# Padding and shifting the weight slots of a two-block transformer kernel, so that weight tiles begin at a chosen distance behind the activation rows modulo 512 bytes

## The chip, the cores and the metric

One core of one Trainium2 chip. The metric is the device time of one execution in microseconds, as the median over runs. The profile is of one execution, traced on that core.

## What is computed

The reference runs two different blocks one behind the other on 256 tokens of width 1024, all in float32. What matters here is which products there are:

```
block 1:  xn = rms_norm(x);  proj = xn @ w_in            # 1024 x 4608
          y  = stick-breaking attention, retention       # small products
          h  = x + (g_sb*y_sb + g_ret*y_ret) @ w_out     # gates: xn @ w_gate
          h  = h + mixture of 16 experts (top 2 of one group of 4)
block 2, two layers, 256 tokens of x and 256 of a context:
          h += 0.5*gate * swiglu(modulate(rms_norm(h)), ffn1_up, ffn1_down)   # 1024 -> 2x2816 -> 1024
          h += gate * (neighbourhood | pool | grouped attention of (a @ w_in)) @ w_out
          h += 0.5*gate * swiglu(..., ffn2_up, ffn2_down)
```

In the second layer's last feed-forward the context is no longer needed, so only 256 tokens are left.

## The kernel before, in words

**Products.** Each large product is made from two-way split operands, so that float32 accuracy is kept with the fast number format: a weight w is split into wH (rounded) and wL (the rest), an activation x into xH and xL, and the sum wH·xH + wH·xL + wL·xH is formed. `gemm` (lines 235 to 244) issues these three matmuls for each block of 128 contraction rows, lines 241, 242 and 243; each has a 128x128 weight tile that TensorE loads (LDWEIGHTS, shown as PEld) and 256, 258 or 512 activation columns that it streams (MATMUL, shown as PE). The next matmul's weight tile is loaded while the matmul before it streams.

**Weights.** `rows` and `load` bring 1 MB of raw weights by DMA from SyncE's queue. `split_w` (lines 220 to 229) takes a slot of 2,048 columns per partition from the pool of weight slots, writes wH into its first half with ScalarE (line 225) and wL into its second half with VectorE or GpSimd (line 228). A slot holds 8 blocks of 128 columns (or 4 of 256, or 2 of 512) in each half, so every 128-column weight tile in a slot begins a multiple of 512 bytes behind the slot's beginning. The slots rotate: 4 in block 1 (`wsp1`), 2 in the mixture of experts (`wspe`), 4 from the first feed-forward to the end (`wsp`).

**Activations.** xH and xL (`setup`, lines 395 and 396) are 8 rows of 512 columns (2,048 bytes) each; tokens of x are columns 0 to 255, the context's are 256 to 511. In the feed-forward (`ffn`, line 569) the up products read xH and xL into `pab`, and the down products read the hidden tiles hH and hL into `pd`. The feed-forward runs over four parts of 6, 6, 6 and 4 hidden blocks (`PARTS`); the first up group of a feed-forward goes through `first` (line 246), which computes the two 256-column halves one after the other while the other half's norm is still being applied; in the very first feed-forward the second part (`EARLY`) has the context's half done already in the mixture of experts (`early_ffn`), so it streams 256 columns. The last down part streams 256 columns at a time. The last feed-forward (`late`) has one 256-column half and two more columns in front of it: 258 columns, beginning at column 254 of the row (line 586). `mix` (line 1308) makes `pj` (from w_in) and `po` (from w_out): 512 columns wide where both halves are needed, with two column groups of w_in again through `first`.

**Order of work.** The program is written as generators that are interleaved by hand (`blend`, `side`, `advance`): while TensorE works on a feed-forward, VectorE computes pieces of the next modulation vectors (`ada`, line 539), a few after each up group. Nothing in that order reads a tile's address.

**Where the tiles lie.** Tiles are placed one behind the other in a partition, in the order of their pools. In the kernel before, in bytes from the partition's beginning:

| tiles | begin at | modulo 512 |
|---|---|---|
| xH, xL, rows of 2,048 bytes | 36,480 and 52,864 | 128 |
| first of 4 weight slots, 8,192 bytes each (block 1, and from the first feed-forward on) | 119,776 | 480 |
| behind these slots: hidden tiles hH, hL (feed-forward), or ysH, ysL (block 1's attention output) | 152,544, 162,784 | 480 |
| `mix`: stacked queries qs (used as weights) / split keys kH, kL (streamed) | 203,168 / 192,736 | 416 / 224 |
| mixture of experts: hidden tiles eH, eL of `early_ffn` | 136,160 | 480 |
| mixture of experts: first of 2 weight slots | 166,432 | 32 |

Between xL and the first weight slot lie, in this order, the small constants, three raw buffers and the scratch pool.

Of the kernel before, what the change touches and what calls it, by code (L numbers as in the profile page):

```python
# [8 lines left out]
F32 = mybir.dt.float32  # L9
F32R = mybir.dt.float32r  # L10
# [19 lines left out]
SB_PACE, RET_PACE, ADA_PACE = 0.8, 0.8, 0.6  # L30
QK_PACE, NA_PACE, OUT_PACE = (2.25, 1.25), (0.75, 0.8), 0.5
NEG = -1e30

_INS = [
    "x", "norm_mix_g", "w_in", "w_gate", "b_gate", "w_sb_out", "w_ret_out", "ret_norm_g", "w_out",
# [134 lines left out]
class Builder:  # L170
    def __init__(self, tc, I, out, ctx):
        self.tc, self.I, self.out, self.ctx = tc, I, out, ctx
        self.nc = tc.nc
        self.const = self.pool("const", 1)
        self.raw = self.pool("raw", 3)
        self.scr = self.pool("scr", 7)
        self.ps = self.pool("ps", 1, space=PSUM)
        self.raw_more, self.raw_loop, self.raw_n = None, None, 0
        self.on_pool, self.mark, self.later, self.spare = 0, None, [], []
        self.pending, self.early, self.norm_a2 = iter(()), iter(()), False  # L180

    def pool(self, name, bufs, **k):
# [34 lines left out]
    def rows(self, w, r0, k, c0, cols):  # L217
        return self.load(w[r0:r0 + 128 * k, c0:c0 + cols].rearrange("(k p) c -> p k c", p=128), k, cols)

    def split_w(self, v):  # L220
        k, cols = v.shape[1], v.shape[2]
        r = lambda t: t[:, :k * cols].rearrange("p (k c) -> p k c", c=cols)
        w = self.wsp.tile([128, 2, 1024], F32R, tag="w", name="w")
        wh, wl = r(w[:, 0, :]), r(w[:, 1, :])
        self.nc.scalar.activation(wh, v, AF.Copy)  # L225
        self.on_pool = (self.on_pool << 1 | self.on_pool >> 3) & 15
        e = self.nc.gpsimd if self.on_pool & 1 else self.nc.vector
        e.tensor_tensor(wl, v, wh.bitcast(F32), ALU.subtract)  # L228
        return wh, wl
# [156 lines left out]
    def setup(self):  # L386
        nc, I = self.nc, self.I
        C = self.const
        sqc = C.tile([128, 896], F32, name="sqc")
        nc.scalar.dma_start(sqc[:, :256], I["k_sq"][:, :256])  # L390
        self.sqc = sqc
        self.ident, self.ones, self.tri, self.perm1, self.perm2, self.flip, self.before = (
            sqc[:, i * 128:(i + 1) * 128] for i in range(7))
        self.h = C.tile([128, KD, T2], F32, name="h")
        self.xH = C.tile([128, KD, T2], F32R, name="xH")
        self.xL = C.tile([128, KD, T2], F32R, name="xL")
        xs = self.token_tiles(I["x"])
        vr = self.vector_rows()
        self.vectors(*vr)
        self.first_norm(xs)  # L400
        self.sT = C.tile([128, KD, 64], F32, name="sT")
        nc.vector.memset(self.sT, 0.0)
# [174 lines left out]
    def ffn(self, l, n, up, dn, vs, side, pace, after):  # L577
# [3 lines left out]
        with ExitStack() as st:  # L581
# [3 lines left out]
            late = len(vs) == 1  # L585
# [4 lines left out]
            f0 = 0  # L590
            for pi, nf in enumerate(PARTS):
                hid = []
                full_n = 256 * len(vs)
                N = 256 if l + n == 0 and pi == EARLY else full_n
                full = slice(0, N)
                for c in range(nf // 2):
                    c0 = (f0 + 2 * c) * 128
                    va = self.rows(up, 0, KD, c0, 256)
                    vb = self.rows(up, 0, KD, NFF * 128 + c0, 256)
                    todo, pabs = [], []  # L600
                    for i in range(2):
# [4 lines left out]
                            p = self.a2("pab")  # L606
                            p = [p[:, 0, :], p[:, 1, :]]
                        pabs.append(p)
                        todo.append((self.split_w(va[:, :, cs]), p[0]))
                        todo.append((self.split_w(vb[:, :, cs]), p[1]))  # L610
                        if pi == 0 and c == 0 and i == 0:
                            continue
                        if late:
# [33 lines left out]
                if pi < len(PARTS) - 1:  # L647
                    for dc in range(4):
                        v = self.rows(dn, f0 * 128, nf, dc * 256, 256)
                        for i in range(2):  # L650
                            w = self.split_w(v[:, :, i * 128:(i + 1) * 128])
                            p = self.mm("pd")
                            self.gemm(p[:, full], w, lambda f: hid[f])
                            for v2 in range(N // S):
                                self.residual(p[:, half(v2)], 2 * dc + i, l, n, v2)
                        for _ in range(pace[1] if N == full_n else 1):
                            next(side, None)
                else:
                    ws = [self.split_w(self.rows(dn, f0 * 128, nf, dc * 256, 256)) for dc in range(4)]
                    for v in sorted(vs):  # L660
                        sq = []
                        for d in range(KD):
# [304 lines left out]
    def moe(self):  # L967
        nc, I = self.nc, self.I
        V = nc.vector
        self.raw_n, self.raws = 0, 7  # L970
        with self.sub("hn", 1) as Q, self.sub("hide", PARTS[EARLY]) as E, self.sub("moe", 1) as P, \
                self.sub("wspe", 2) as self.wsp, self.sub("moew", 1) as W, self.sub("rawm", 4) as self.raw_more:
            hH = [Q.tile([128, 1024], F32R, name=f"hnH{t}") for t in range(2)]
# [332 lines left out]
    def mix(self, l):  # L1306
        nc, I = self.nc, self.I
        full = l == 0
        w_in = I["w_in_2"][l]
        NX = 512 if full else 256  # L1310
        with self.sub("mx", 1) as P, self.sub("mxw", 2) as W:
# [2 lines left out]

            def weights(c):
                v = self.rows(w_in, 0, KD, c * 256, 256)
                return [self.split_w(v[:, :, i * 128:(i + 1) * 128]) for i in range(2)]

            first = []
            self.on_pool = 5  # L1320
# [94 lines left out]
            def most():  # L1415
                for c in range(4):
                    v = self.rows(I["w_out_2"][l], 256, 6, c * 256, 256)
                    for i in range(2):
                        w = self.split_w(v[:, :, i * 128:(i + 1) * 128])
                        n = NX  # L1420
                        if full and c == 3:
                            n = S
# [313 lines left out]
    def run(self):  # L1736
# [3 lines left out]
        self.moe()  # L1740
        self.wsp = self.pool("wsp", 4, reuse_waits="tile")

        for l in range(2):
            side = self.adas((0, 1), (0, 2)) if l == 0 else self.adas((1, 2))
            self.ffn(l, 0, I["ffn1_up_2"][l], I["ffn1_down_2"][l], (1, 0) if l == 0 else (0, 1), side, (5, 3),
# [33 lines left out]
```

## Time and profile before

| | |
|---|---|
| runs | 2264.26, 2265.17, 2266.32 us; median 2265.17 us |
| the profiled execution | 2263.28 us, of it the span of the trace 2261.5 us |
| TensorE busy | 97% of the span, mean granted clock 0.99 |
| VectorE, ScalarE, GpSimd busy | 64%, 36%, 7% |
| moved by DMA | 395.91 MB, 175 GB/s over the span |

How to read it: a MATMUL's time in the trace runs from its start to its result and overlaps the next one's, so the rate of TensorE is read from the distance of two starts, which is called the **pitch** below. In a stretch where one group of matmuls follows without a gap, it is the length of the stretch divided by the number of starts. PEclk is the granted clock as a share of 2.4 GHz.

### The profile page before, as it was taken

What the parts mean: (1) busy time and instruction counts of PE and PEld (TensorE: products, weight loads), DVE (VectorE), ACT (ScalarE), POOL (GpSimd) and SP (SyncE); (2) the same over time, 40 slices, a digit from 0 to 9 for tenths busy, and PEclk for the clock granted to TensorE, in tenths of its full rate; (3) what the DMA queues carried; (4) which work ended last, traced back from release to release, by engine and by line L of the source; (5) the groups of instructions that cost most, each with busy time, mean ns of one, the idle gap of its engine ahead of it and who ended that gap; (6) DMA issues with size and microseconds to landing.
All of it is one profiled execution on the core that took longest, in us unless ns stands there. A gap on an engine that the chain in (4) does not pass through costs nothing.

```text
span 2261.5 us, 32422 instructions
## 1 busy us (share of the span) xinstructions
PE 2190.4 (97%) x13295; PEld 1796.4 (79%) x13295; DVE 1441.2 (64%) x2516; ACT 816.3 (36%) x1256; POOL 164.8 (7%) x160
## 2 busy tenths in 40 slices
PE   8999999997999999999999999999999999899998
PEld 8789974543689877977887777788878888879998
DVE  5656852321489787766688777648863345877666
ACT  4564531201233322447542222224222223475443
POOL 0200100000000000430110000010000003212000
PEclk9999999999999999999999999999999999999999
DMA  8674869998856654320335555333553222317551
GB/s 257 212 246 131 263 222 346 362 386 351 321 175 214 215 178 149 86 66 29 121 120 190 175 183 180 114 131 121 184 180 98 89 68 70 102 34 226 185 177 47
DMA packets 285461, 395.91 MB, mean 175 GB/s; under 512 B 18156, under 2 KB 220540, under 8 KB 285180
## 3 DMA queue, kind: packets, MB, share of 16 engines
q1 hardware_dynamic: 284288, 392.33, 51.8%
q8 instruction: 106, 1.74, 0.3%
q0 software_dynamic: 576, 1.18, 0.2%
q14 instruction: 47, 0.39, 0.0%
q10 hardware_dynamic: 444, 0.27, 0.0%
HBM read 392.71 MB, written 1.05 MB: 174 GB/s over the span
## 4 chain that ended last, share of the span: by engine, by line
PE 69%; DVE 4%; ACT 1%; POOL 1%; issue 1%; ACTq 0%; DVEq 0%; POOLq 0%
PE pab L241 12%; PE pab L243 12%; PE pab L242 12%; PE pd L241 6%; PE pd L242 6%; PE pd L243 6%; PE pj L242 2%; PE pj L241 2%; PE pj L243 2%; PE egu L1150 1%; PE aT L1632 1%; PE as L1603 1%; PE ao L1649 1%; PE ada_ps L521 1%; PE po L241 1%; DVE xL L330 1%
## 5 line engine op out<-in xcount | busy, mean ns | idle before, releaser
L225 ACT ACTIVATE w<-raw 128x1024 fp32r<-128x1024 f32 (+2 forms) x432 | 425.4, 990 | 686.5 <-PE pd L243 240.5
L228 DVE TENSOR_TENSOR w<-raw,w 128x1024 fp32r<-128x1024 f32 (+2 forms) x422 | 479.9, 1147 | 191.6 <-ACT w L225 189.7
L242 PE MATMUL pab<-xL,w 128*128 128x512 f32 (+2 forms) x1600 | 552.5, 346 | 2.1 <-DVE xL L1474 1.0
L243 PE MATMUL pab<-xH,w 128*128 128x512 f32 (+2 forms) x1600 | 551.9, 345 | 1.4 <-POOL w L228 1.4
L241 PE MATMUL pab<-xH,w 128*128 128x512 f32 (+2 forms) x1600 | 553.0, 346 | 0.1
L241 PEld LDWEIGHTS pab<-xH,w 128*128 128x128 f32 x1600 | 303.2, 190 | 54.3 <-issue 9.9
L242 PEld LDWEIGHTS pab<-xL,w 128*128 128x128 f32 x1600 | 303.1, 190 | 46.9 <-issue 4.1
L243 PEld LDWEIGHTS pab<-xH,w 128*128 128x128 f32 x1600 | 303.4, 190 | 45.2 <-issue 4.1
L539 DVE SCALAR_TENSOR_TENSOR acc<-raw,sT,acc 128x512 f32<-128x512 f32 x420 | 284.9, 747 | 0.0
L241 PE MATMUL pd<-hH,w 128*128 128x512 f32 (+1 forms) x800 | 267.2, 336 | 0.3 <-ACT hH L232 0.2
L242 PE MATMUL pd<-hL,w 128*128 128x512 f32 (+1 forms) x800 | 267.1, 335 | 0.0
L243 PE MATMUL pd<-hH,w 128*128 128x512 f32 (+1 forms) x800 | 266.4, 334 | 0.0
L241 PE MATMUL pj<-xH,w 128*128 128x256 f32 (+1 forms) x816 | 250.9, 309 | 12.1 <-DVE qra L1531 4.7
L242 PE MATMUL pj<-xL,w 128*128 128x256 f32 (+1 forms) x816 | 245.9, 302 | 7.3 <-DVE xL L330 6.5
L243 PE MATMUL pj<-xH,w 128*128 128x256 f32 (+1 forms) x816 | 245.0, 301 | 0.5 <-DVE w L228 0.5
L241 PEld LDWEIGHTS pj<-xH,w 128*128 128x128 f32 x816 | 156.0, 192 | 27.2 <-DVE qra L1531 5.5
L241 PEld LDWEIGHTS pd<-hH,w 128*128 128x128 f32 x800 | 151.2, 190 | 20.4 <-ACT fs L636 3.4
L242 PEld LDWEIGHTS pj<-xL,w 128*128 128x128 f32 x816 | 156.9, 192 | 13.2 <-DVE xL L330 7.8
L686 DVE SCALAR_TENSOR_TENSOR h<-pd,gmod,h 128x256 f32<-128x256 f32 x224 | 100.9, 479 | 103.8 <-PE pd L243 103.5
L243 PEld LDWEIGHTS pd<-hH,w 128*128 128x128 f32 x800 | 151.5, 190 | 16.8 <-issue 1.7
L242 PEld LDWEIGHTS pd<-hL,w 128*128 128x128 f32 x800 | 151.8, 190 | 15.4 <-DVE hL L233 0.2
L243 PEld LDWEIGHTS pj<-xH,w 128*128 128x128 f32 x816 | 156.5, 192 | 5.7 <-DVE w L228 0.8
(388 smaller groups left out, 2449.3 us busy)
## 6 DMA issues: line engine op xcount, KB each, us to landing
raw<-ffn_up SPq DMA_DIRECT2D x94, 1024.0 KB, 5.3
raw<-w_ada SPq DMA_DIRECT2D x72, 1024.0 KB, 5.3
raw<-ffn_down SPq DMA_DIRECT2D x52, 768.0 KB, 4.7
raw<-w_in SPq DMA_DIRECT2D x32, 1024.0 KB, 5.4
raw<-w_exp_gate SPq DMA_DIRECT2D x32, 1024.0 KB, 9.5
raw<-w_exp_up SPq DMA_DIRECT2D x32, 1024.0 KB, 9.3
raw<-w_exp_down SPq DMA_DIRECT2D x32, 1024.0 KB, 8.2
raw<-w_gate SPq DMA_DIRECT2D x8, 1024.0 KB, 6.0
```

Of the source, the lines that this page charges most:

```text
L225: self.nc.scalar.activation(wh, v, AF.Copy)
L228: e.tensor_tensor(wl, v, wh.bitcast(F32), ALU.subtract)
L241: mm(o, wH[:, k, :], aH, start=(first and k == 0), stop=False)
L242: mm(o, wH[:, k, :], aL, start=False, stop=False)
L243: mm(o, wL[:, k, :], aH, start=False, stop=(last and k == n - 1))
L330: nc.vector.scalar_tensor_tensor(lo, t, B(j), hi.bitcast(F32), ALU.add, ALU.subtract)
L521: mm(ps[g * 32:(g + 1) * 32, :], self.unit[:, 31 - r:63 - r], acc[v], start=(u < 2), stop=(u > 3))
L539: ins = V.scalar_tensor_tensor(acc[v], w[:, g, :], s, acc[v], ALU.mult, ALU.add)
L686: self.nc.vector.scalar_tensor_tensor(hs, p, self.gmod[:, l, n, d, v:v + 1], hs, ALU.mult, ALU.add)
L1150: mm(pr[a * 64:a * 64 + 64, m, :], xg[p // 2][:, q * 2 + kk, es[a] % 4 * 64:es[a] % 4 * 64 + 64], w[:, a, kk * 512:(kk + 1) * 512], start= ...
L1603: mm(o[:, c], qs, x[i][:, c], start=(i == 0 and not (near and c.start == 0)), stop=(i == 1))
L1632: nc.tensor.transpose(T[:, j * 128:(j + 1) * 128], e[:, a, j * 128:(j + 1) * 128], self.ident)
```

## The change

A weight slot becomes 64 columns (256 bytes) longer. `split_w` places wH and wL at an offset `off` of 0, 16 or 24 columns in the slot (0, 64 or 96 bytes), which the caller chooses by the number of columns that will be streamed: 0 for 512, 16 for 256, 24 for the late feed-forward's 258; in the mixture of experts it is 0. A constant tile of 40 columns (160 bytes) that nothing uses is placed behind xL.

```
+LEAD, W_PAD, OFF_256, OFF_258, OFF_512 = 40, 64, 16, 24, 0
...
+        self.w_off = OFF_256
...
-    def split_w(self, v):
+    def split_w(self, v, off=None):
+        off = self.w_off if off is None else off
         k, cols = v.shape[1], v.shape[2]
         r = lambda t: t[:, :k * cols].rearrange("p (k c) -> p k c", c=cols)
-        w = self.wsp.tile([128, 2, 1024], F32R, tag="w", name="w")
-        wh, wl = r(w[:, 0, :]), r(w[:, 1, :])
+        w = self.wsp.tile([128, 2048 + W_PAD], F32R, tag="w", name="w")
+        wh, wl = (r(w[:, off + a:off + a + 1024]) for a in (0, 1024))
...                                                     # setup
         self.xL = C.tile([128, KD, T2], F32R, name="xL")
+        C.tile([128, LEAD], F32, name="lead")
...                                                     # ffn
+                off_up = OFF_512 if N == 512 else OFF_258 if late else OFF_256
+                off_dn = OFF_512 if N == 512 else OFF_256
...
-                        todo.append((self.split_w(va[:, :, cs]), p[0]))
-                        todo.append((self.split_w(vb[:, :, cs]), p[1]))
+                        todo.append((self.split_w(va[:, :, cs], off_up), p[0]))
+                        todo.append((self.split_w(vb[:, :, cs], off_up), p[1]))
...
-                            w = self.split_w(v[:, :, i * 128:(i + 1) * 128])
+                            w = self.split_w(v[:, :, i * 128:(i + 1) * 128], off_dn)
...                                                     # the last down part
-                    ws = [self.split_w(self.rows(dn, f0 * 128, nf, dc * 256, 256)) for dc in range(4)]
+                    ws = [self.split_w(self.rows(dn, f0 * 128, nf, dc * 256, 256), OFF_256) for dc in range(4)]
...                                                     # moe
-        self.raw_n, self.raws = 0, 7
+        self.raw_n, self.raws, self.w_off = 0, 7, 0
...                                                     # mix: w_in
-                return [self.split_w(v[:, :, i * 128:(i + 1) * 128]) for i in range(2)]
+                off = OFF_512 if width(2 * c) == 512 else OFF_256
+                return [self.split_w(v[:, :, i * 128:(i + 1) * 128], off) for i in range(2)]
...                                                     # mix: w_out
-                        w = self.split_w(v[:, :, i * 128:(i + 1) * 128])
+                        w = self.split_w(v[:, :, i * 128:(i + 1) * 128], OFF_512 if full else OFF_256)
...                                                     # run, behind the mixture of experts
+        self.w_off = OFF_256
```

## Rows read from the trace of the kernel before

**Rows 1.** The profile page: its span, TensorE's share and granted clock in 40 slices, and the chain of work that ended last, by engine.

```profile
span 2261.5 us, 32422 instructions
PE 2190.4 (97%) x13295; PEld 1796.4 (79%) x13295; DVE 1441.2 (64%) x2516; ACT 816.3 (36%) x1256; POOL 164.8 (7%) x160
PEclk9999999999999999999999999999999999999999
PE 69%; DVE 4%; ACT 1%; POOL 1%; issue 1%; ACTq 0%; DVEq 0%; POOLq 0%
```

**Rows 2.** Groups of instructions with shapes kept apart, TensorE. Shown is the first of `gemm`'s three lines for each output and width; lines 242 and 243 have the same counts. The mean is a matmul's own time, not the pitch.

```profile
L241 PE MATMUL pab<-xH,w 128*128 128x512 f32 x864 | 344.0, 398 | 0.0
L241 PE MATMUL pj<-xH,w 128*128 128x256 f32 x704 | 203.6, 291 | 6.6 <-ACT w L225 3.2 <-DVE ra L733 1.6 <-DVE h L479 0.9
L241 PE MATMUL pd<-hH,w 128*128 128x512 f32 x384 | 150.2, 391 | 0.0
L241 PE MATMUL pd<-hH,w 128*128 128x256 f32 x416 | 117.0, 286 | 0.3 <-ACT hH L232 0.2
L241 PE MATMUL pab<-xH,w 128*128 128x256 f32 x384 | 110.9, 291 | 0.1
L241 PE MATMUL pab<-xH,w 128*128 128x258 f32 x352 | 98.1, 280 | 0.0
L241 PE MATMUL pj<-xH,w 128*128 128x512 f32 x112 | 47.3, 422 | 5.4 <-DVE qra L1531 4.7 <-DVE qc L1515 0.7
L241 PE MATMUL po<-xH,w 128*128 128x256 f32 x104 | 30.7, 295 | 0.2 <-DVE h L686 0.2
L241 PE MATMUL po<-xH,w 128*128 128x512 f32 x36 | 14.6, 407 | 0.0
```

**Rows 3.** The timeline of a feed-forward's 512-column up product, at its third part: start, duration, engine, line.

```profile
1743.06 0.39 PE L243 MATMUL pab<-xH,w 128*128 128x512 f32 x1
1743.06 0.19 PEld L241 LDWEIGHTS pab<-xH,w 128*128 128x128 f32 x1
1743.29 0.39 PE L241 MATMUL pab<-xH,w 128*128 128x512 f32 x1
1743.29 0.19 PEld L242 LDWEIGHTS pab<-xL,w 128*128 128x128 f32 x1
```

**Rows 4.** Busy time of TensorE in stretches of up products, of the instructions that read or write `pab` alone: window, its length, PE busy and the number of matmuls in it, granted clock, DMA share, GB/s. Each window opens and closes 0.01 us outside the first and the last start of a stretch without a gap. In the first and third one matmul that was still running at the opening is counted too, so the starts are 191, 288, 211 and 288. The widths are 256, 512, 258 and 258 columns.

```profile
716.36:738.92 22.56, 22.56 (x192) 1.00 0.75 240
1742.58:1809.84 67.26, 67.25 (x288) 1.00 0.30 97
2068.19:2093.64 25.45, 25.45 (x212) 1.00 0.80 256
2111.60:2145.43 33.83, 33.82 (x288) 1.00 0.58 185
```

**Rows 5.** The same view of `pd`: two stretches of `early_ffn` in the mixture of experts (256 columns, 17 and 19 starts), one of a 512-column down product (144 starts), one of a 256-column down product in the late feed-forward (116 starts).

```profile
432.87:434.72 1.85, 1.85 (x18) 1.00 1.04 416
438.72:440.86 2.14, 2.14 (x20) 1.00 1.02 314
1810.05:1842.50 32.45, 32.44 (x144) 1.00 0.17 50
2149.21:2163.03 13.82, 13.82 (x117) 1.00 0.64 206
```

**Rows 6.** The same view of `pj` in block 1, 256 columns: 167 starts of a product that reads xH and xL, and 37 of one that reads the attention output ysH and ysL.

```profile
25.58:45.09 19.51, 19.51 (x168) 1.00 0.90 305
223.59:227.92 4.33, 4.33 (x38) 1.00 0.52 182
```

**Rows 7.** The same view of `as`, the score products of the second layer's grouped attention: 512 key columns streamed against stacked queries, 8 starts.

```profile
1975.65:1977.28 1.63, 1.62 (x8) 1.00 0.00 0
```

**Rows 8.** Busy time of all engines by stage: block 1, the later mixture of experts, the busiest feed-forward stage of VectorE, the late feed-forward. Columns: window, length, PE, PEld, DVE, ACT, POOL busy with counts, granted clock, DMA share, GB/s.

```profile
12.00:285.00 273.00, 264.44 (x2129) 242.70 (x2129) 183.68 (x311) 140.56 (x190) 27.37 (x23) 1.00 0.68 221
410.00:598.00 188.00, 167.13 (x886) 82.64 (x886) 46.30 (x75) 24.66 (x40) 0.00 (x0) 0.97 0.95 364
598.00:703.60 105.60, 105.60 (x557) 90.03 (x558) 89.26 (x168) 29.82 (x41) 0.00 (x0) 0.98 0.61 199
2055.00:2237.00 182.00, 180.66 (x1499) 178.73 (x1498) 130.83 (x246) 87.33 (x119) 5.19 (x6) 1.00 0.54 174
```

**Rows 9.** Who TensorE waited for between 1140 and 2250 us, longest first.

```profile
PE pj L242 <- DVE xL L330: 4.8, 2, 3.2
PE qrp L1513 <- DVE qrw L1525: 2.0, 1, 2.0
PE pab L243 <- POOL w L228: 1.4, 1, 1.4
```

**Rows 10.** The groups of `split_w`'s two writes on the page: line, engine, operation, count, busy and mean, idle before and what ended it.

```profile
L225 ACT ACTIVATE w<-raw 128x1024 fp32r<-128x1024 f32 (+2 forms) x432 | 425.4, 990 | 686.5 <-PE pd L243 240.5
L228 DVE TENSOR_TENSOR w<-raw,w 128x1024 fp32r<-128x1024 f32 (+2 forms) x422 | 479.9, 1147 | 191.6 <-ACT w L225 189.7
```

## The prediction, made before the changed kernel was run

> **What bounds the kernel now.** I read the page first: TensorE is busy for 97% of the span at nearly full clock, and it carries most of the chain that ended last [rows 1]. So the question is how fast TensorE gets through its own matmuls. The groups by shape [rows 2] give the number of matmuls for each output and width, but their mean (398 ns for 512 columns) is a latency. The pitch must come from stretches without a gap [rows 4 to 7], all at granted clock 1.00. The timeline [rows 3] shows what runs together: the weight load of the next matmul starts in the same hundredth of a microsecond as the running matmul. So each stream of activation columns runs beside a read of 512 bytes of the next weight tile, and the two addresses can matter.
>
> I call the distance from the streamed row to the weight tile loaded beside it, modulo 512 bytes, the **phase**. From the table of addresses: the first slot lies 119,776 - 36,480 = 83,296 = 162 x 512 + 352 bytes behind xH, slots are 8,192 = 16 x 512 long, rows 2,048. So every product on xH and xL has phase 352 (360 in the late feed-forward, whose row begins 8 bytes before a multiple of 512 from xH). hH, ysH and the slots are all at 480: phase 0. In the mixture of experts, eH has (32 - 480) mod 512 = 64. Grouped scores have 416 - 224 = 192.
>
> Now the pitches, window less 0.02 us over starts less one:
> - 512 columns: phase 352, 67.24/287 = 234.3 ns [rows 4]; phase 0, 32.43/143 = 226.8 ns [rows 5]; phase 192, 1.61/7 = 230.0 ns [rows 7].
> - 256 columns: phase 352, 19.49/166 = 117.4 ns [rows 6] and 22.54/190 = 118.6 ns [rows 4], I take 118.0; phase 0, 13.80/115 = 120.0 ns [rows 5] and 4.31/36 = 119.7 ns [rows 6]; phase 64, 1.83/16 = 114.4 and 2.12/18 = 117.8 ns [rows 5], I take 116.1.
> - 258 columns at phase 360: 25.43/210 = 121.1 and 33.81/287 = 117.8 ns [rows 4].
>
> Phase 0 costs the same for ysH in block 1 as for hH at the end, so it is not the output or the stage that sets the pitch. But equal phases differ by up to 3.4 ns at 256 columns, so phase is not all. For 512 columns the gap of 7.5 ns is clear.
>
> **The change part by part.** The unused 160 bytes move all that lies behind xL: the first slot's distance becomes 83,456 = 163 x 512, phase 0. The slot's new length of 8,448 = 16 x 512 + 256 gives slots two and four phase 256. So 512-column products get 0 or 256, 256-column ones with offset 64 bytes get 64 or 320, late ones (96 + 8) 104 or 360. Four longer slots push what lies behind by 160 + 1,024 = 1,184 bytes, and hH stays in phase with the even slots: down products also get 0 or 256 (512 columns) and 64 or 320 (256 columns). In the mixture of experts the first slot is at phase 416 + 160 = 64 from xH.
>
> The unknown is the price of phases 256, 320 and 104, which no row has. At 512 columns phase 256 lies between 192 (230.0) and 352 (234.3); if the pattern repeats every 256 bytes it is 226.8. The bounds I take are 226.8 and 234.3. The nearest row, 192, speaks for a middle price. My reason for the repeat all the same: at phase 0, 256 more columns cost 226.8 - 120.0 = 106.8 ns, so 512 columns alone are 213.6 ns, and the excess is 13.2 ns at phase 0 and 20.7 at 352. In a load's time the stream runs through twice the bytes of the weight tile, so their distance shifts by 512 bytes and each phase meets each distance once; phase 0 puts the meeting at the load's two ends. If only that one meeting cost time, phase 0 should be left with little of it. A rest of more than half looks rather like two meetings, 256 bytes apart, of which phase 0 (and then 256 too) moves one to the ends. This is an argument, not a row. I take the repeat as the likeliest: 256 as 0, 320 as 64, 104 as 360.
>
> The sum on that case:
> - 512 columns on xH, xL: 3 x (864 + 112 + 36) = 3,036 matmuls [rows 2] x (234.3 - 226.8) = -22.8 us. 512-column down products go from 0 to 0 or 256: 0.
> - 256-column down products of the feed-forwards, 3 x 416 = 1,248 [rows 2] x (120.0 - 116.1) = -4.9 us.
> - 256 columns on xH, xL in slots with offset 64: of `pj` 2,112 less the 288 that `first` runs in `mix` with offset 0, of `po` 312 less 72 (the last two output blocks of the first layer), of `pab` the 288 of the part `EARLY`: 2,352 x (118.0 - 116.1) = -4.5 us. 1,632 of these are in block 1, where TensorE also waits for VectorE's and ScalarE's work [rows 2, 8]; of their 3.1 us I count half: -3.0 us.
> - 256-column halves that `first` runs with weights placed for 512 columns (576 of `pab`, 288 of `pj`), and the 72 of `po`: 936 go from 118.0 to the 119.9 of phase 0: +1.8 us.
> - 258 columns: 360 or its repeat, 0.
> - Mixture of experts: `early_ffn` runs beside expert weights whose DMA share is 0.95 [rows 8]. I cost it at nothing; cover gone, its 288 + 144 matmuls are worth 1 us.
> - `split_w`'s writes keep their size. ScalarE has 36% and VectorE 64% of the span, idle ahead of them is a wait for TensorE or for each other [rows 1, 10]. A write slowed by its new address has bounds of zero and, at one tenth of 990 and 1147 ns, 0.1 us for each tile under a TensorE that takes 24 x 234.3 ns = 5.6 us for it: 0. No DMA, wait or instruction is added or moved; SyncE's and GpSimd's queues keep their order. Slots and later pools overlap the same earlier pools as before, all of which TensorE has left by then: 0.
>
> Together -28.9 us. What is late next: VectorE. In its busiest feed-forward stage it has 89.3 of 105.6 us [rows 8]; that stage shortens by 3 us, so it stays under 90%. At the changes of stage TensorE waits for norms and queries [rows 9], and a wait for VectorE does not shrink with the matmuls ahead of it. I give back 3 us: **-26 us**. Against the profiled execution's 2263.28 us this is 2237.3 us; the runs' median lies 1.9 us above it, so **2239 us**.
>
> The trace has two prices for two phases. The Trainium skill, page "TensorE: Matmul & The Clock Gate", Part 2 (step-by-step), says that TensorE has two independent read ports into SBUF and that loading the next tile's weights takes no read bandwidth from the running matmul. By that rule the sum would be 0; the 234.3 beside 226.8 ns at one clock does not agree.
>
> **The rivals.**
> - *B: the repeat is not there, only phase 0 is cheap.* Odd slots at 256 then cost 232 (between 230.0 and 234.3), those at 320 the 118.0 of phase 352. Half of the 3,036: -11.4, the other half 1,518 x 2.3 = -3.5; half of 1,152 down products at 512 columns lose 576 x 5.2 = +3.0; 256-column down products 624 x 3.9 + 624 x 2.0 = -3.6; the rest -1.5 + 0.9. Sum -16, less 2 for waits: -14, **2251 us**. For it: 230.0 and 234.3 stand on both sides of 256. With 256 at the full 234.3 it is -9: 2256 us.
> - *C: the phase is not the cause*, and pitch follows something that goes with hH: **2265 us**, no change. For it: the unequal pitches at equal phase. Against: `pj`, `po` and `pab` differ in output, stage and length and share phase 352; ysH and hH share 0 and 119.7 to 120.0 ns. This is also what the rule on the two ports would give.
> - *D, slower: phases 256 and 320 are the bad ones.* All odd slots lose: 1,518 + 576 + 1,176 + 624 + 468 = 4,362 matmuls. The even slots gain about 13 us, so it decides from 13/4,362 = 3.0 ns a matmul on, and is slower by 0.2% from 4.0 ns. At 6 ns: -13 + 26 = +13 us, **2278 us**. For it: 3.4 ns appear between stretches of one phase. Against: 192 and 352 enclose 256 and are no worse than today.
>
> **How the numbers follow.** The main case gets 0.54: the one price that carries it is measured on hundreds of matmuls, half of it on an assumed repeat. B gets 0.31, C 0.07, D 0.08. The low end is the main case with 114.4 instead of 116.1 ns at 256 columns (some -5) and nothing given back: 2231 us. The high end is B with phase 256 at today's price, 2256 us. This leaves out C and D, 0.15. A measurement of this kernel can tell about 0.2% (4.5 us) from no change. The first two cases are faster by more: 0.85; C is the same: 0.07; D slower: 0.08.
>
> **What would show it.** Right: 512-column stretches of `pab` at 227 ns in all slots, `pd` at 512 unchanged, late `pd` at 116, granted clock as now, no new wait of TensorE over 3 us. B: 512-column pitches alternate by slot, 24 at 227 and 24 at 232, and `pd` at 512 rises. C: nothing moves. D: alternate slots above today's 234.3. The prediction fails too if the matmuls come faster and the stages do not shorten, with VectorE's waits in their place.

## The result, and the profile of the changed kernel

The changed kernel takes **2237.67 us** (median of 4 runs, 2234.53 to 2246.69); the kernel before, run beside it, 2265.74 us. The ratio is 0.9877, with an interval of 0.986 to 0.9894. The forecast was 2239 us in a range of 2231 to 2256. Run twice more, the same kernel took 2241.63 and 2240.58 us; the median of all 12 executions is 2240.2 us, so the change is worth about 25 us. The profiled execution took 2246.69 us and is the slowest of its four: a stretch of it is compared with before only where the execution doesn't matter, and for the rest the profile of experiment 7 ("third run", 2240.12 us) is used.

The page of the changed kernel, against [rows 1]: the span fell by 16.6 us and TensorE's busy time by 21.2 us, at the same share, with the same 13,295 matmuls and a mean granted clock of 0.986 beside 0.990. VectorE's share of the chain rose from 4% to 5%.

```profile
span 2244.9 us, 32423 instructions
PE 2169.2 (97%) x13295; PEld 1791.1 (80%) x13295; DVE 1443.3 (64%) x2516; ACT 817.0 (36%) x1256; POOL 162.5 (7%) x160
PEclk9999999999999999999999999999999999999999
PE 69%; DVE 5%; ACT 1%; issue 1%; POOL 1%; ACTq 0%; DVEq 0%; POOLq 0%
```

The stretches of `pab`, as in [rows 4]: window, length, PE busy and count, granted clock, DMA share, GB/s. Each opens and closes 0.01 us outside the first and last start; the starts are 288 (512 columns, 0 and 256 in turn), 191 and 96 (256 columns, 64 and 320), 127 (256-column halves of `first`, 0 and 256), 211 and 288 (258 columns, 104 and 360).

```profile
1724.21:1789.28 65.07, 65.06 (x288) 1.00 0.31 100
713.79:735.36 21.57, 21.57 (x192) 1.00 0.74 240
701.17:712.38 11.21, 11.20 (x96) 1.00 0.84 282
608.53:623.65 15.12, 15.12 (x128) 1.00 0.46 159
2051.58:2076.33 24.75, 24.75 (x212) 1.00 0.82 262
2094.07:2128.84 34.77, 34.76 (x288) 1.00 0.55 181
```

With the prediction's arithmetic: 512 columns 65.05/287 = **226.7 ns**, where before had 234.3; 256 columns at 64 and 320 21.55/190 = 113.4 and 11.19/95 = 117.8; halves at 0 and 256 15.10/126 = 119.8; 258 columns 24.73/210 = 117.8 and 34.75/287 = 121.1, as before.

The same view of `pd`, against [rows 5]: a 512-column down product (144 starts, phases 0 and 256) and two 256-column ones of the late feed-forward (116 starts each, 64 and 320).

```profile
1789.49:1821.92 32.43, 32.42 (x144) 1.00 0.16 50
2080.40:2093.96 13.56, 13.56 (x117) 1.00 0.63 210
2132.62:2145.67 13.05, 13.05 (x117) 1.00 0.66 218
```

512 columns stay at 32.41/143 = 226.6 ns in slots of both phases; 256 columns fall from 120.0 to 13.54/115 = 117.7 and 13.03/115 = 113.3 ns.

Busy time by stage, against the last two of [rows 8], in the same columns: VectorE's busiest feed-forward stage is 1.5 us shorter with the same VectorE work, and TensorE is still busy in all of it.

```profile
597.00:701.10 104.10, 104.10 (x558) 89.87 (x558) 89.26 (x168) 29.85 (x41) 0.00 (x0) 0.98 0.61 202
2039.06:2220.30 181.24, 179.56 (x1496) 177.61 (x1495) 130.32 (x246) 86.66 (x118) 4.53 (x6) 1.00 0.54 175
```

TensorE's waits in the last half of the span (1130 to 2235 us), against [rows 9]. The first and the third are new at the head of the list. The two writes of `split_w` [rows 10] have means of 990 and 1145 ns, as before.

```profile
PE rb L309 <- DVE nr_y L297: 2.4, 2, 2.1
PE pj L245 <- DVE xL L333: 2.0, 2, 1.8
PE ss L317 <- DVE sqa L351: 2.0, 1, 2.0
PE qrp L1520 <- DVE qrw L1532: 2.0, 1, 2.0
PE pab L246 <- POOL w L231: 1.4, 1, 1.4
...
```

### The profile page after: what moved, and what is told of

Its sections match the earlier page's. It is cut to its first block, busy times and chain, and to the rows that moved or that the text cites. A ratio compares the mean times of both kernels' runs of the same rounds, so it can differ in the third digit from the quotient of the medians.

```text
span 2244.9 us, 32423 instructions
## 1 busy us (share of the span) xinstructions
PE 2169.2 (97%) x13295; PEld 1791.1 (80%) x13295; DVE 1443.3 (64%) x2516; ACT 817.0 (36%) x1256; POOL 162.5 (7%) x160
## 4 chain that ended last, share of the span: by engine, by line
PE 69%; DVE 5%; ACT 1%; issue 1%; POOL 1%; ACTq 0%; DVEq 0%; POOLq 0%
PE pab L244 12%; PE pab L245 12%; PE pab L246 12%; PE pd L244 6%; PE pd L245 6%; PE pd L246 6%; PE pj L245 2%; PE pj L244 2%; PE pj L246 2%; PE egu L1156 1%; PE aT L1639 1%; PE as L1610 1%; PE ao L1656 1%; PE ada_ps L525 1%; DVE xL L333 1%; PE po L244 1%
## 5 line engine op out<-in xcount | busy, mean ns | idle before, releaser
L231 DVE TENSOR_TENSOR w<-raw,w 128x1024 fp32r<-128x1024 f32 (+2 forms) x422 | 479.0, 1145 | 184.1 <-ACT w L228 182.2
L245 PE MATMUL pab<-xL,w 128*128 128x512 f32 (+2 forms) x1600 | 546.2, 342 | 2.2 <-DVE xL L1481 1.0
L244 PE MATMUL pab<-xH,w 128*128 128x512 f32 (+2 forms) x1600 | 546.4, 342 | 0.2
L246 PE MATMUL pab<-xH,w 128*128 128x512 f32 (+2 forms) x1600 | 544.8, 341 | 1.4 <-POOL w L231 1.4
L246 PEld LDWEIGHTS pd<-hH,w 128*128 128x128 f32 x800 | 151.1, 189 | 16.6 <-issue 1.7
```

Source lines behind the costliest of these rows:

```text
L244: mm(o, wH[:, k, :], aH, start=(first and k == 0), stop=False)
L245: mm(o, wH[:, k, :], aL, start=False, stop=False)
L246: mm(o, wL[:, k, :], aH, start=False, stop=(last and k == n - 1))
```

## The experiments

### 1. A scan of phases in one kernel

```
-        off = self.w_off if off is None else off
+        self.turn = (getattr(self, 'turn', -1) + 1) % 8
+        off = 8 * self.turn
```

Every weight tile takes the next of eight offsets (0, 32, ... 224 bytes), whatever its product asks for.

> The changed kernel, but the offset in the slot no longer goes by the number of columns: it steps through 0, 32, 64, ... 224 bytes from one weight tile to the next, so every width meets sixteen phases, 0 to 480 in steps of 32. Theory A (the pitch goes by the phase modulo 256): one curve for each width, the same for the two halves of the 512 bytes; 512 columns near 227 ns at phases 0 and 256 and 230 to 235 ns at 64 to 224 and 320 to 480; 256 columns near 120 ns at 0 and 256 and 113 to 118 ns at 64 and 320. Rival C (the pitch goes with the streamed tile or the stage, not with the phase): no curve, 512 columns at 227 ns at every phase in this kernel too. The time itself is of no use here; on theory A it lies between the two kernels, 2245 to 2265 us.

It took 2265.92 us. One 512-column stretch of `pab`, one window for each weight tile's 24 loads; phases modulo 256 in order 32, 64, 96, 128, 160, 192, 224, 0:

```profile
1750.80:1756.40 5.60, 5.60 (x26) 1.00 0.20 69
1756.40:1761.99 5.59, 5.59 (x25) 1.00 0.00 0
1761.99:1767.61 5.62, 5.62 (x26) 1.00 0.27 81
1767.61:1773.20 5.59, 5.59 (x25) 1.00 0.36 110
1773.20:1778.81 5.61, 5.61 (x26) 1.00 0.40 140
1778.81:1784.31 5.50, 5.50 (x25) 1.00 0.00 0
1784.31:1789.91 5.60, 5.60 (x25) 1.00 0.27 83
1789.91:1795.35 5.44, 5.44 (x25) 1.00 0.47 149
```

A length over 24 is the pitch: 5.44/24 = 226.7 ns at phase 0, 5.50/24 = 229.2 at 192, and 233 to 234 for the six others, while the clock stays at 1.00 and the DMA's share goes from 0 to 0.47 without a trace in the lengths. So phase alone moves the pitch from one weight tile to the next. Means over the whole trace, of pitches between consecutive starts, worked out by phase modulo 256 (ns):

| columns | 0 | 32 | 64 | 96 | 128 | 160 | 192 | 224 |
|---|---|---|---|---|---|---|---|---|
| 512 | 227.5 | 233.2 | 233.4 | 233.8 | 232.6 | 233.4 | 229.4 | 233.3 |
| 256 | 119.5 | 118.1 | 115.9 | 118.8 | 118.7 | 119.8 | 117.3 | 117.4 |

It follows that C falls, and that the two widths want different phases: 0 is the cheapest for 512 columns and nearly the dearest for 256.

The scan meets eight of the sixteen phases modulo 512, not all as was expected: the offsets go round in eight and the slots in four, so each offset always falls into a slot of the same parity (phases 0, 288, 64, 352, 128, 416, 192, 480). That the price repeats after 256 bytes is not shown here but by the even and odd slots of the changed kernel and by experiment 3.

### 2. The shift of 160 bytes alone

```
+        C.tile([128, 40], F32, name="lead")
```

This is the kernel before with the unused tile and nothing else: slots of 8,192 bytes, every weight tile at phase 0 (8 in the late feed-forward), hidden tiles as before.

> The kernel before with nothing but the unused 160 bytes behind xL: slots keep 8,192 bytes, so every weight tile from the first feed-forward on has phase 0 from xH and from the hidden tiles, for all widths. Theory A: 512-column products on xH and xL fall from 234.3 to 226.8 ns (3,036 x 7.5 = -22.8 us); 256-column products on xH rise from 118.0 to 119.8 ns (3,288 x 1.8 = +5.9 us, half of block 1's part hidden, so +4.5); hidden products stay at 226.8 and 120.0. Sum -18 us, 2245 to 2250 us, and 9 to 11 us slower than the changed kernel. Rival C: no change, 2265 us. Rival (the longer slot or the offsets inside it matter for other reasons, such as where ScalarE and VectorE write): less than half of the gain, 2255 us or more.

2249.79 us (2247.21 to 2253.7), ratio 0.9939 (0.9922 to 0.9955). A 512-column stretch of `pab` (288 pitches) and a 258-column one (288):

```profile
1729.03:1794.31 65.28, 65.28 (x288) 1.00 0.31 100
2094.16:2128.46 34.30, 34.30 (x288) 1.00 0.57 184
```

65.28/288 = 226.7 ns, with phase 0 in every slot; 34.30/288 = 119.1 ns at phase 8. One tile of 160 bytes that nobody reads gives some 15 of the 25 us; the rest came with the padding, which lets the 256-column products have a phase of their own.

### 3. 512-column products at phase 96 and 352

```
-LEAD, W_PAD, OFF_256, OFF_258, OFF_512 = 40, 64, 16, 24, 0
+LEAD, W_PAD, OFF_256, OFF_258, OFF_512 = 40, 64, 16, 24, 24
```

> The changed kernel with one constant changed: weight tiles for 512 columns begin 96 bytes into the slot instead of 0, phase 96 or 352. Theory A: 352 was measured at 234.3 ns and 96 is its repeat, so the 3,036 products on xH and xL go back to 234.3 and, for the first time, the 1,152 products on hidden tiles as well: 4,188 x 7.5 = +31 us; the halves that are computed one after the other with these weights go from 119.8 to about 118 (936 x -1.8 = -1.7). Sum +29 us over the changed kernel, 2267 us, no better than the kernel before. Rival B or any theory in which 96 is not like 352: alternate tiles of 24 matmuls at different pitches, and half of that or less. Rival C (hidden tiles are cheap by themselves): the hidden products stay at 226.8, +21 us at most.

2272.68 us (2268.9 to 2276.51), ratio 1.0034 (1.0023 to 1.0045): 31 us slower than the changed kernel on the same chip, by one constant. Nine tiles of `pab` (216 pitches) and seven of a 512-column `pd` (126), each in slots of 96 and 352 by turns:

```profile
1755.76:1806.36 50.60, 50.60 (x217) 1.00 0.26 85
...
1821.82:1851.34 29.52, 29.52 (x127) 1.00 0.16 54
```

50.60/216 = 234.3 ns and 29.52/126 = 234.3 ns: `pd`, which had 226.8 in the kernel before, now pays the same, so the output and its stage have no part in it, and 96 is priced as 352. It came out 6 us over what was expected. In its profiled execution the two changes into `mix` (last down part, then `first`) are 2.9 - 1.7 + 1.4 + 3.4 = 6.0 us longer than before, of which more below.

### 4. The changed kernel again

No edit.

> The changed kernel once more, unaltered. Its profiled execution took 2246.69 us while its other three took 2234.53 to 2238.54 us, against a spread of 3 us in the kernel before. Theory M: at phases 64 and 320 a stretch of 256-column matmuls runs in one of two locked pitches, 113.4 or 117.8 ns, chosen anew in each execution and stretch; 3,600 such matmuls make up to 16 us. Then this profile has the same two pitches but in other stretches, and the executions spread over 5 us or more. Rival W: the slow execution lost its 8 us around the start of the second layer's mix, where the granted clock fell to 0.5 four times between 1897 and 1949 us; then this profile shows the same pitches in the same stretches and differs there.

2241.63 us (2240.08 to 2249.66), ratio 0.9909 (0.9885 to 0.9932); its profiled execution took 2240.08 us. Both theories hold in part. 256- and 258-column stretches at one phase do change between two pitches from execution to execution (117.8 and 113.4, 121.1 and 117.8), but largely cancel between these two; of the 6.6 us between the two profiled executions some 5 lie between 1886 and 1905 us, at the change into the second `mix`. There the granted clock fell to 0.5 (1.2 GHz) at 1887.0 us and again at 1897.3 us in the one, and not before 1911.8 us in the other; TensorE had stood 2.1 us for `nr_y` just before in both, and between the two falls it waited 2.0 us for `sqa` in the slow one alone. (Counted from the first instruction, as all times here, the four falls that the expectation names lie between 1887 and 1942 us.)

### 5. The halves at phase 64 too

```
+                    off_c = OFF_256 if pi == c == 0 and not late else off_up
...
-                        todo.append((self.split_w(va[:, :, cs], off_up), p[0]))
-                        todo.append((self.split_w(vb[:, :, cs], off_up), p[1]))
+                        todo.append((self.split_w(va[:, :, cs], off_c), p[0]))
+                        todo.append((self.split_w(vb[:, :, cs], off_c), p[1]))
...
-                off = OFF_512 if width(2 * c) == 512 else OFF_256
+                off = OFF_512 if width(2 * c) == 512 and c not in (6, 4) else OFF_256
...
-                        w = self.split_w(v[:, :, i * 128:(i + 1) * 128], OFF_512 if full else OFF_256)
+                        w = self.split_w(v[:, :, i * 128:(i + 1) * 128], OFF_512 if full and c < 3 else OFF_256)
```

The 936 matmuls that the prediction had getting slower are given 64 and 320.

> The changed kernel with three more products placed by the columns that they really stream: the up products that the feed-forwards compute half after half (576 matmuls), the two column groups of w_in treated so (288) and the last column group of the first layer's w_out (72) get the 64 bytes of 256 columns instead of 0. Theory A: these 936 go from 119.8 ns (phases 0 and 256) to about 115.3 (64 and 320): -4.2 us against the changed kernel in the same job, 2235 to 2239 us. Rival (these stretches wait for the norm of the other half, so their pitch is worth nothing): no difference, within 1.5 us of the changed kernel. Rival D' (the gain is lost again in waits at the stage's end): pitches as said, time the same.

2239.9 us (2238.41 to 2241.89) against 2240.58 for the changed kernel on the same chip: 0.7 us, within the scatter, not the 4 us that were expected of their pitch. The pitch did as said: a stretch of halves in the first feed-forward (36 pitches), 4.24/36 = 117.8 ns, and 115.9 on the mean of the feed-forwards' halves, where the changed kernel has 119.7. The stages do not follow. First the stretch, of `pab` alone; then the three feed-forward stages that open with halves (length, PE busy, granted clock):

```profile
608.24:612.48 4.24, 4.24 (x38) 1.00 1.07 371
...
595.78:622.49 26.71, 26.71 (x213) 0.92 0.71 236
1136.21:1163.36 27.15, 25.50 (x201) 0.94 0.24 79
1516.27:1541.63 25.36, 24.37 (x200) 1.00 0.26 84
```

192 matmuls by 3.8 ns would be 0.7 us in each. Against the changed kernel's 26.88, 26.98 and 26.26 us they are 0.2 us shorter, 0.2 longer and 0.9 shorter. The second still has its wait of 1.4 us for a weight split, and a granted clock of 0.94 where the changed kernel has 1.00: by itself that can cost 0.06 x 27.15 = 1.6 us, an estimate, which is more than the 0.7 that was to come. These halves exist to fill time while a norm is still being applied; that a faster matmul gains nothing there for this reason is likely, but not shown, since the clock differs too.

### 6. A fine scan around 0 and 64

```
-        off = self.w_off if off is None else off
+        self.turn = (getattr(self, 'turn', -1) + 1) % 8
+        off = (2, 4, 62, 60, 12, 14, 18, 20)[self.turn]
```

> The changed kernel with the offset stepping through 8, 16, 248, 240, 48, 56, 72 and 80 bytes from one weight tile to the next. It measures how wide the cheap place at phase 0 is for 512 columns and whether 64 is the cheapest for 256. If the price goes by a broad meeting of two streams, 8 and 248 bytes are as cheap as 0 (227 to 228 ns) and 16 and 240 between (229 to 231); if it goes by equal addresses to the byte, 8 and 248 already cost 232 or more. For 256 columns the first expects 48 to 80 all near 115 to 116 ns, the second a single cheap value at 64. No forecast for the time, 2245 to 2265 us.

2270.99 us. The same stretch as in the first scan, three windows of it, phases modulo 256 of 248, 240 and 8:

```profile
1758.01:1763.61 5.60, 5.60 (x26) 1.00 0.00 0
1763.61:1769.09 5.48, 5.48 (x26) 1.00 0.26 67
...
1791.44:1796.98 5.54, 5.54 (x26) 1.00 0.48 155
```

At 512 columns 248 costs 5.60/24 = 233.3 ns, 240 228.3, 8 230.8; 16, 48, 56 and 72 cost 233.3 to 233.5 on the mean, 80 232.0. The cheap place at 0 is only a few bytes wide, and not symmetric: 248 is dear between 0 and 240. Neither theory of the expectation fits, since 8 lies between the prices that the two gave for it. At 256 columns (means) 72 costs 118.4, 56 117.9, and the others 117.9 to 118.8: 64 with its 115.9 stands out from its neighbours, but it is not the only cheap place, since 8 costs 116.6.

### 7. The changed kernel a third time, beside 5 and 6

No edit.

> The changed kernel unaltered, as the yardstick for the placement by halves on the same chip: 2235 to 2245 us by its eight executions so far. Theory W: the profile shows the same pitches as before within 0.3 ns at 512 columns; what is different between its executions lies in the 256-column stretches and in the granted clock at the changes of stage.

2240.58 us (2239.52 to 2241.18), ratio 0.9889 (0.9872 to 0.9905). From first matmul to first matmul of the stages that carry the prediction's terms, this execution less the one profiled before:

| stages | said, us | measured, us |
|---|---|---|
| 11 stages of `pab`, 512 columns (2,592 matmuls) | -19.4 | -19.0 |
| `pj` and `po`, 512 columns (444) | -3.3 | +0.6 - 0.5 - 0.3 = -0.1 |
| `pd` at 256 columns: all but the two parts ahead of `mix` (864) | -3.4 | -3.8 |
| the same, the two parts ahead of `mix` (384) | -1.5 | **+1.7 + 3.0 = +4.6** |
| block 1's `pj` (256) | -1.5 | -3.0 |
| the part `EARLY`, `pab` (288 at 256 columns) | -0.5 | -1.1 |
| `first` at the opening of feed-forwards (576) | +1.1 | +0.4 |

Two rows stand out. The first is the part ahead of `mix`, of both layers. In the kernel before TensorE is busy in all of both (length, PE busy, granted clock; the changed kernel's lines stand in 8 to 10):

```profile
909.27:933.10 23.83, 23.83 (x200) 1.00 0.06 15
1887.70:1911.73 24.03, 24.03 (x199) 1.00 0.19 53
```

The timeline of the changed kernel (third run), ahead of the first `mix`:

```profile
917.53 1.06 ACT L228 ACTIVATE w<-raw 128x1024 fp32r<-128x1024 f32 x1 [1.69 <-PE pd L246]
...
918.66 2.34 POOL L231 TENSOR_TENSOR w<-raw,w 128x1024 fp32r<-128x1024 f32 x1 [1.38 <-ACT w L228]
918.73 2.29 DVE L297 SCALAR_TENSOR_TENSOR nr_y<-nr_a,nr_y 128x1 f32<-128x1 f32 x1
...
921.08 0.32 PE L309 MATMUL rb<-sqc,nr_y 128*128 128x128 f32 x1 [2.07 <-DVE nr_y L297]
```

The same place in the kernel before:

```profile
928.40 2.43 POOL L228 TENSOR_TENSOR w<-raw,w 128x1024 fp32r<-128x1024 f32 x1 [1.44 <-ACT w L225]
...
928.42 0.15 DVE L294 SCALAR_TENSOR_TENSOR nr_y<-nr_a,nr_y 128x1 f32<-128x1 f32 x1
...
928.50 0.44 PE L306 MATMUL rb<-sqc,nr_y 128*128 128x128 f32 x2
```

`nr_y` is the last step of a norm, one number a partition. Beginning 0.02 us after GpSimd's weight split it takes 0.15 us; 0.07 us after it, it lasts as long as the split, 2.29 us, and TensorE, whose queue has the norm's transpose next, stands for 2.07 us. It happens again ahead of the second `mix`, and in all the profiles here it goes by the distance of the two starts: 6 steps that began 0.02 to 0.03 us after such a split (before, experiments 1 and 2) took 0.14 to 0.15 us, 12 that began 0.06 to 0.08 us after it took 2.28 to 2.30 us. The Trainium skill, page "SBUF — State Buffer", section "Who interferes with whom", says that a VectorE instruction with two inputs in SBUF contends with a GpSimd instruction that reads SBUF; the trace agrees for the step that began 0.07 us behind, 2.29 us in place of 0.15, and shows no contention for the one 0.02 us behind.

Of the second part's 3.0 us about half is the clock's: in its last 5.5 us the granted clock is 0.69. In the profile of experiment 4, where it stays at 1.00 there, the two parts are 1.2 and 1.5 us longer than before, 2.6 in all, with the same two waits of 2.1 us.

What brought the step there can be read from experiments 2 and 3. With the lead alone, whose 256-column down products keep 120 ns, the longest `nr_y` is 0.71 us; at phase 96, where only the 256-column products are faster, it is 2.29 us and TensorE's wait on it 4.6 us in total. That points to the faster down products. It is not settled, for a few hundredths of a microsecond decide: in the first scan these parts run at 117.8 and 117.9 ns and the step takes 0.14 us, in the fine scan at 118.3 and 118.2 ns and it takes 2.29 us.

The second row is `pj` and `po`: their pitch did fall (234 to 229.5 ns on the mean), and TensorE's busy time in the longest of these stages with it, from 111.4 to 109.5 us (at mean granted clocks of 0.97 and 0.99, so a part of that is the clock's). But the stage has a wait for ScalarE's exponentials, first before, then here:

```profile
PE as L1603 <- ACT e L1614: 0.8, 1, 0.8
...
PE as L1610 <- ACT e L1621: 3.5, 1, 3.5
```

In the other two profiled executions of the changed kernel it is 1.9 and 0.9 us, and the stage takes 117.07 and 115.86 us, against 117.09 here and 116.47 before. So of the 240 x 7.5 = 1.8 us that were said for this stage at most 0.6 came back, and the wait alone does not account for the rest: with 1.9 us of it the stage is no shorter, at a granted clock of 0.97 in place of 0.99.

### 8 to 10. GpSimd's splits moved to other places

GpSimd takes every second of the first four weight splits of `mix`. Three kernels move these, so that none stands beside the norm's last step:

```
-            self.on_pool = 5
+            self.on_pool = 3
```

This is experiment 8, with the third and fourth of the four on GpSimd; in 9 the number is 1, and only the last is.

> The changed kernel, and of mix's first four weight splits the second is done by VectorE and the third by GpSimd (before: VectorE, GpSimd, VectorE, GpSimd). Theory G (part of the gain is given back since the faster down product brings GpSimd's second split of 2.3 us in front of the norm's last small VectorE step, which then takes 2.3 us instead of 0.15 while TensorE waits 2.1 us for it, in both layers): that step takes 0.15 us at both places, TensorE's waits for it fall from 4.5 to under 0.5 us in all, and the kernel gets 2 to 4 us faster than the changed one, 2236 to 2238 us, if the split that is now VectorE's (1.2 us) isn't in the way. Rival (the norm's chain is late for its own length, GpSimd is only there at the same time): the waits stay, no difference. Rival (the third split on GpSimd then stands in front of the apply steps): the step is short, but xL's steps take 2 to 3 us more, no difference or slower.

> As the kernel with the third split moved to GpSimd, but VectorE does the first three and GpSimd the last alone. Theory G: the norm's last step takes 0.15 us in both layers too; VectorE gets one more split of 1.2 us ahead of mix. 2235 to 2239 us; better than the other order if a GpSimd split anywhere ahead of the apply steps costs more than 1.2 us on VectorE, worse if VectorE's own queue is what the apply steps wait for. Rival: no difference to the changed kernel, 2240 us.

Experiment 10 is 5 and 8 together.

> The placement by halves and the new order of the splits together. Theory G with the pitches: if the placement by halves (4.2 us of TensorE's time) was lost to the same late norms, part of it comes out now: 2232 to 2237 us. Rival (the halves wait for the apply steps of the other half whatever the splits do): the same as with the new order alone, 2236 to 2240 us.

They took 2238.43, 2240.43 and 2240.19 us on one chip: ratios 0.9873 (0.9855 to 0.9891), 0.9885 (0.9867 to 0.9902) and 0.9883 (0.9865 to 0.9902), none apart from the changed kernel's 0.9889. Experiment 8 shows why. The parts ahead of the two `mix`, and `first` behind each, first in the changed kernel (third run; length, busy time of PE, PEld, DVE, ACT and POOL, granted clock, DMA share, GB/s), then in 8 (PE alone):

```profile
899.84:925.35 25.51, 23.44 (x201) 23.21 (x200) 16.70 (x46) 9.40 (x16) 10.35 (x12) 1.00 0.16 51
925.35:952.02 26.67, 24.91 (x209) 24.66 (x207) 21.08 (x51) 11.14 (x20) 13.01 (x12) 1.00 0.47 105
1863.99:1890.98 26.99, 24.92 (x199) 24.46 (x198) 17.89 (x42) 11.54 (x19) 11.06 (x13) 0.94 0.25 79
1890.98:1943.67 52.69, 45.70 (x340) 44.28 (x338) 42.41 (x83) 22.36 (x41) 22.29 (x23) 0.90 0.44 122
```

```profile
900.90:923.74 22.84, 22.84 (x201) 1.00 0.12 37
923.74:954.35 30.61, 27.00 (x208) 0.94 0.43 106
1865.04:1888.81 23.77, 23.77 (x200) 1.00 0.23 70
1888.81:1943.13 54.32, 46.53 (x341) 0.91 0.46 127
```

The down parts now run without a gap, 2.7 and 3.2 us shorter (the second at a clock of 1.00 in place of 0.94, too), and `first` is 3.9 and 1.6 us longer: of 5.9 us, 0.3 are left. The waits of the whole span, of experiment 8, tell what took the place:

```profile
PE pj L245 <- DVE xL L333: 8.8, 7, 2.3
```

The changed kernel has 4.3 us there, in 2 waits. The `nr_y` steps are short again (0.71 us at most), and the writes of xL, the next work of the same norm on VectorE, meet more of the splits: at each `mix` two of them, usually 0.48 us long, take 2.0 and 3.1 to 3.3 us beside one, where the changed kernel's third run has a single one of 3.06 us. At the first `mix` TensorE's busy time for `first` is 2.1 us longer too, at a granted clock of 0.94. What `first` waits for in these kernels is the chain from norm to xL on VectorE beside GpSimd; moving the splits moved the wait.

## Why the prediction was right, step by step

- **What bounds the kernel.** Right. TensorE's pitch in stretches without a gap was the place to look; the matmuls' own durations (`pab`, a mean of 342 ns on the page) would have told nothing of a change of 7.5 ns.
- **The phase sets the pitch.** Right, and now shown: 226.7 beside 234.3 ns at one clock and one instruction, for `pab` and `pd` alike, with an offset alone changed (1, 3). C had 0.07; the rule of two independent read ports (the Trainium skill, page "TensorE: Matmul & The Clock Gate", Part 2), by which it would have come true, does not agree with this. It is the distance and not the weight tile's own address: in the kernel before `pab` and `pd` loaded from the same slots, at 234.3 and 226.8 ns.
- **The price of phases 256, 320, 104.** Right: 256 as 0 (means of 226.7 at 256 and 227.0 at 0 in the changed kernel's `pab`), 320 as 64 (115.5, 115.7), 104 as 360 (119.5, 119.4), 96 as 352 (experiment 3). That refutes B and D, which had 0.31 and 0.08. But the reason given for the repeat is not what was found. A meeting of two addresses that phase 0 puts at a load's ends would make the neighbours of 0 nearly as cheap as 0. Measured are 233.4 at 248, 228.3 at 240, 230.7 at 8 and a plateau of some 233 elsewhere, with another cheap place at 192. The nearest row, 192, was no guide either: 230.0 and 234.3 stood on both sides of 256, and the price between was below both, since the curve is no slope. The argument's premise, that the stream runs through twice the tile's bytes in a load's time, stands in no row either: a load lasts 0.19 us in [rows 3], beside a pitch of 0.234. The repeat was a guess that held.
- **The terms of the sum.** 512 columns of `pab`: -19.0 of the -19.4. 256 columns at 64 were taken at 116.1 ns and have 115.6, a little better. Halves: their 1.8 ns came as said, and weigh little: taking them back in experiment 5 changed the time by 0.7 us, within the scatter.
- **What is late next.** This is the step that was mis-sized. The give-back was put at 3 us, on the waits at the changes of stage, where it is; it is some 9: 6 us at the down parts ahead of `mix` (+4.6 where -1.5 was said, of which about 1.5 us the lower clock; +2.6 in experiment 4), and 3 of the 444 matmuls of `pj` and `po`, whose pitch fell by 4.5 ns only and whose longest stage met a longer wait for ScalarE. That wait, 3.5 us in the third run, is also over the 3 us that were named as the most for a new one. The prediction looked at VectorE's share (89 of 105 us) and saw room, rightly for that stage, though it shortened by 1.5 us and not by the 3 that were said: it has only 192 matmuls of 512 columns. The wait came from one small VectorE step held by a GpSimd instruction, in a stage whose VectorE share is two thirds (16.7 of 25.5 us). No share shows that. "A wait for VectorE does not shrink" was also too mild: this one grew, from nothing to 2 us, twice.
- **Why the total came out all the same.** Against that, block 1 gave 1.5 us more than counted, the part `EARLY` 0.6 more, the late up products 0.9, `first` in the feed-forwards 0.7, the other down parts 0.4. Of these the late up products are that execution's luck: nearly all their weight tiles held 117.6 to 117.8 ns (mean 117.7), where the kernel before has a mean of 118.5 and the changed kernel's other two profiles 119.3 and 119.4 at the same phases. Between the two profiled executions (2263.28 and 2240.12) lie -23.2 us, where -26 was said: a give-back some 6 us too small and gains some 4 us too small, in opposite directions, hide in the 3 us.

What stays open: why 0 and 192 are cheap at 512 columns and 64 at 256, that is, what the two reads share; and why a 256-column stretch of one phase holds one of two pitches. No run took the two streams apart.

## What to carry to other kernels

Where TensorE is the bound, work out the pitch, start to start, of each product and width in stretches without a gap, and compare them: unequal prices for equal work at one granted clock are a lead, and where the weight tile lies against the streamed row is one to try, by a scan of offsets inside one kernel, since each weight tile then is its own experiment. Choose the good place for each width that streams by itself. And when matmuls become faster, go through the changes of stage for small steps that now land beside another engine's long instruction: there the gain is given back, and a busy share does not show it.

## What the runs showed of the hardware that was not expected

- TensorE's pitch at fixed clock depends on the distance between streamed row and loaded weight tile modulo 256 bytes: 226.7 to 234.3 ns at 512 columns, 115.5 to 119.8 at 256, with cheap places only a few bytes wide (0: 227, 248: 233.4, 240: 228.3) and different ones for the two widths.
- 256-column stretches at one phase hold one of two pitches without a break (113.4 or 117.8 ns; at 258 columns 117.8 or 121.1), and the same stretch of the same kernel may take the other in the next execution.
- A VectorE step on one number a partition took 2.29 us in place of 0.15 when it began 0.07 us after a GpSimd split of 2.34 us, and 0.15 us when it began 0.02 us after one; so it was in all 12 and all 6 cases of the runs.
